# A hybrid decoder's MLPs: each pair of feature tiles of the first product alternates with the second product of four earlier tiles

## Chip, core and metric

One core of one Trainium2 chip runs the whole kernel. The metric is the device time of one launch in microseconds (us). Three runs of the kernel before the change took 1593.59, 1597.19 and 1599.14 us; the median is 1597.19 us.

## The reference

The program is one step of a two-layer decoder trunk on T = 544 tokens (512 of a prompt, 8 x 4 of samples), width 1024, in float32. Layer 0 mixes with mLSTM and GLA heads, layer 1 with an SSD scan; each mixer is followed by a squared-ReLU MLP with 4096 features. The change is in the two MLPs alone:

```
def _mlp(x, w1, w2):
    return jnp.square(jax.nn.relu(x @ w1)) @ w2

x = _layernorm(DN_ALPHA * x + _mlp(x, w1[l], w2[l]), g, b)     # for both layers
```

## The kernel before

Everything is held transposed: features on the 128 partitions, tokens along the row, in two halves of 272 tokens. The 4096 features of an MLP are 32 tiles of 128. A product in float32 is made of three matmuls: each operand x is split into a rounded part (hi, a cast on ScalarE) and the rest (lo, a subtraction on VectorE), and hi*hi, hi*lo, lo*hi are added up in PSUM. So each weight block, 128 x 1024, is loaded by a DMA from SyncE's queue into a buffer `wraw` (three of them), cast by ScalarE into `whi` (L148) and subtracted by VectorE into `wlo` (L149).

The first product makes hidden tiles (function `act`, L474): ReLU on ScalarE (L478), the square on VectorE or GpSimd (L479), then the split into `hh` and `hlo` (`split`, L262 to 264: cast on ScalarE, subtraction on VectorE). Eight hidden tiles are kept at a time (`bufs=8`). The second product (`dense`, L328) takes them as its moving operand: for an output block b of 128 features and one token half, 3 matmuls for each hidden tile run into one PSUM bank (`psd`, three banks), and VectorE adds the sum into the residual stream `xf` (`residual`, L370 for the first group, L372 after).

`mlp` (L432) goes through four groups c of eight feature tiles. In group 0 the first six tiles (`HEADM`) are plain products, done for token half 0 of all six and then for half 1. Meanwhile `take_sums` (L444) prepares sums of the activations, t1 to t4. All the other tiles come in pairs (`pair`, L482): seven quarter products of 12 matmuls each in place of eight, as in Strassen's method, with weight sums that GpSimd forms (`_pair` of the weight stream, L172 to 175, into `wsum`) and that are split like the rest (L183, L184). The quarters run in the order a11, s2, s3, s1, a12, a22, s4. A pair m gives four half tiles. Tile m+1, half 1 (called c22) is complete after the fourth quarter, tile m, half 0 after a12, tile m+1, half 0 (c21) after a22, tile m, half 1 (c12) after s4. The half from a12 is squared on VectorE, the other three on GpSimd.

After the pairs of a group the eight output blocks follow, each over the group's eight hidden tiles (24 matmuls for each half): `phase(8, hrhs, KT, residual(c == 0))`. In group 3 the last seven blocks go as one group, half by half, and the layer norm starts behind each half.

What sets the order of the work: TensorE keeps the order of the code (`manual_schedule`). For the other engines a scheduler writes a fixed order for each engine while the program is built, and each engine then executes its own queue strictly in that order. The weight stream (`WeightStream`, L101) prepares blocks ahead: `next` (L192) emits as many blocks as fit in six buffers (`HLB` = 5 and `HLM` = 1), where a pair counts as three; a pair's fourth piece (a22) has a single buffer of its own, and so has `wsum`.

Of the kernel before, what the change touches and what calls it, by code (L numbers as in the profile page):

```python
# [33 lines left out]

W = dict(dec=12, gates=400, sc=16, lev=12, v=8, kd=10, out=33, end=12, c0=15, u=11, s=16, ml=12, dt=238, sg=72, sx=14, sq=26, so=48, l0=12, l1=12, v0=60, v1=55)
LEVELS = (64, 32, 16, 8, 4, 2, 1)

# [63 lines left out]
class WeightStream:  # L101
# [14 lines left out]

    @staticmethod
    def _size(block):
        return 1 if len(block) == 2 else 3
# [4 lines left out]
    def _emit(self, between=None):  # L124
        nc = self.nc
        phase, *srcs = self.blocks[self.done]
        self.done += 1
        if len(srcs) == 2:
            with self.tc.high_priority():
                self.tiles.append(self._pair(phase, *srcs))  # L130
            return
        src, = srcs
        _, kt, _ = src.shape
        pool = self._pool(phase)
        with self.tc.high_priority(), ExitStack() as after:

            for i in self.cut:
                if i is not None:
                    after.enter_context(self.tc.issue_after(i))
            self.cut = [None, None]  # L140
            w = self.raw.tile([P, kt, P], F32, tag="wraw", name="wraw")
            hi = pool.tile([P, kt, P], F32R, tag="whi", name="whi")
            lo = pool.tile([P, kt, P], F32R, tag="wlo", name="wlo")
# [8 lines left out]
            self.tiles.append((hi, lo))  # L152

    def _pool(self, phase):
        if phase == self.extra_phase:
# [53 lines left out]
def trunk_kernel(ctx, tc, a, stages=("ab", "mlp0", "ssd", "mlp1")):  # L209
# [19 lines left out]
    for st in stages:  # L229
        if st == "ab":  # L230
            for w in [a["ab_gate"]] + [a["ab_in"][b] for b in range(24)]:
                ws.plan("ab", w)
            for b in range(8):
                ws.plan("abo", a["ab_out"][b])
        elif st == "ssd":
            for w in [a["ssd_dt"]] + [a["ssd_in"][b] for b in range(40)]:
                ws.plan("ssd", w)
            for w in [a["ssd_out"][b] for b in range(16)]:
                ws.plan("ssdo", w)
        else:  # L240
            l = int(st[3])
            for c in range(4):
                n = HEADM if c == 0 else 0
                for b in range(n):
                    ws.plan(st, a["mlp_w1"][l, c * 8 + b])
                for b in range(n, 8, 2):
                    ws.plan(st, a["mlp_w1"][l, c * 8 + b], a["mlp_w1"][l, c * 8 + b + 1])
                for b in range(8):
                    ws.plan(st, a["mlp_w2"][l, c, b])


    xf = [None, None]
# [179 lines left out]
    def mlp(l, phase_, outer, xp, out):  # L432
# [29 lines left out]
        for c in range(4):  # L462
            hid = {}

            def place(m):
                if m not in hid:
                    hid[m] = (pool.tile([P, T], F32R, tag="hh", name="hh", bufs=8),
                              pool.tile([P, T], F32R, tag="hlo", name="hlo", bufs=8))
                return hid[m]

            def hr():
                return pool.tile([P, TH], F32, tag="hr", name="hr", bufs=6)

            def act(m, hf, x, E, r=None):  # L474
                c0, c1 = HALVES[hf]
                h = place(m)
                r = hr() if r is None else r
                S.activation(r, x, AF.Relu)  # L478
                E.tensor_tensor(r, r, r, ALU.mult)  # L479
                split(h[0][:, c0:c1], h[1][:, c0:c1], r)  # L480

            def pair(m):  # L482
                w = ws.next()
                pa, pb, pc, pe = (x[:, :TH] for x in (psd.tile([P, 512], F32, tag="d", name="psd"), pm("psd"),
                                                      psd.tile([P, 512], F32, tag="d", name="psd"), pm("psd")))
                hp = tc.high_priority
                z, c22, c21, c12 = (hr() for _ in range(4))
                quarter(w["a11"], bt["b11"], pa, True)
                with hp():
                    S.copy(z, pa)  # L490
                quarter(w["s2"], bt["t2"], pb, True)
                with hp():
                    V.tensor_tensor(z, z, pb, ALU.add)
                quarter(w["s3"], bt["t3"], pc, True)
                with hp():
                    V.tensor_tensor(c22, z, pc, ALU.add)  # L496
                quarter(w["s1"], bt["t1"], pe, True)
                with hp():
                    V.tensor_tensor(c22, c22, pe, ALU.add)
                quarter(w["a12"], bt["b21"], pa, False)  # L500
                with hp():
                    act(m + 1, 1, c22, G, c22)
                    act(m, 0, pa, V)
                quarter(w["a22"], bt["t4"], pc, False)
                with hp():
                    V.tensor_tensor(c21, z, pc, ALU.add)
                    act(m + 1, 0, c21, G, c21)
                quarter(w["s4"], bt["b22"], pe, False)
                with hp():
                    V.tensor_tensor(c12, z, pe, ALU.add)  # L510
                    act(m, 1, c12, G, c12)

            def hrhs(k, hf):
                c0, c1 = HALVES[hf]
                return hid[k][0][:, c0:c1], hid[k][1][:, c0:c1]

            if c == 0:
                phase(HEADM, xrhs, KT, lambda m, hf, ps: act(m, hf, ps, V), head=HEADM)
                take_sums()
            for m in range(HEADM if c == 0 else 0, 8, 2):  # L520
                if (c, m) == (3, 6):
                    ws.lend(None, None, 0)
                pair(m)
            if c < 3:
                phase(8, hrhs, KT, residual(c == 0))
            else:
                own.close()
                ws.lend(outer.enter_context(tc.tile_pool(name="hlx" + phase_, bufs=HLX, reuse_waits="tile")), phase_, HLX)
                phase(8, hrhs, KT, residual(False, xp, out is not None), tail=TAIL,
                      after=lambda hf: launch(layernorm(hf, 2 * l + 1, xp, out)))  # L530


    def ab(pool):
# [1300 lines left out]
```

## Time and profile before

| what | value |
|---|---|
| median of the three runs | 1597.19 us |
| the profiled execution, its own time | 1592.68 us |
| its span, first to last instruction | 1591.0 us |
| mean granted TensorE clock | 0.983 |
| matmuls of the program | 11621 |
| first MLP's products, us from the span's start | about 331 to 717 |
| second MLP's products | about 1209 to 1574 |

The span is the time between the first and the last instruction of the profiled execution; its own time is 1.7 us longer. In the profile PE is TensorE's matmuls, PEld its weight loads, DVE is VectorE, ACT is ScalarE, POOL is GpSimd, SP is SyncE. A row such as "psd<-hh,whi" names the tile written, then those read. In the rows of groups, "x1024 | 297.6, 291 | 6.3 <-ACT hh" reads: 1024 instructions, 297.6 us busy, 291 ns each, and 6.3 us in which the engine idled just before them, ended mostly by ScalarE's write of `hh`. Matmuls overlap: the duration of one is longer than the step from one start to the next.

### The profile page before, as it was taken

The numbers are of one execution on the slowest core, as the hardware profiler recorded it, in microseconds if no ns is written. First come the engines' busy times: TensorE is split into PE (matmuls) and PEld (weight loads), VectorE is DVE, ScalarE is ACT, GpSimd is POOL, SyncE is SP. The second block draws the span as 40 slices with busy tenths as digits, with TensorE's granted clock in tenths as the row PEclk, the third lists the DMA queues.
The fourth block names the chain that finished last, engine by engine and source line by source line (L and its number), as shares of the span: only waits on it lengthen the run. The fifth ranks groups of instructions, "written<-read, shape, count | busy, mean of one in ns | idle before, by whom it ended". The sixth has DMA issues, their size and how long they took to land.

```text
span 1591.0 us, 29243 instructions
## 1 busy us (share of the span) xinstructions
PE 1504.7 (95%) x11621; PEld 1446.0 (91%) x11621; DVE 1060.7 (67%) x1871; ACT 734.6 (46%) x1569; POOL 586.7 (37%) x603
## 2 busy tenths in 40 slices
PE   8899999989999999999799999999898999999997
PEld 7799989989989999999787788899888999999996
DVE  4963566777383655757798978667669647474654
ACT  6543555344251433525585666645234435162433
POOL 0320323353242434344353463543245233343421
PEclk9999999999999999999999999999999999999999
DMA  6121122503142241415447667363221414132221
GB/s 221 58 81 63 44 94 87 176 26 119 38 138 70 59 146 41 154 50 187 101 130 242 207 176 251 94 217 118 67 61 46 133 41 133 54 113 87 67 80 57
DMA packets 81488, 172.10 MB, mean 108 GB/s; under 512 B 14696, under 2 KB 39144, under 8 KB 81096
## 3 DMA queue, kind: packets, MB, share of 16 engines
q1 hardware_dynamic: 45384, 141.20, 28.0%
q10 hardware_dynamic: 33376, 18.42, 4.6%
q0 software_dynamic: 2592, 10.62, 1.7%
q8 instruction: 91, 1.49, 0.4%
q14 instruction: 45, 0.37, 0.1%
HBM read 153.48 MB, written 16.73 MB: 107 GB/s over the span
## 4 chain that ended last, share of the span: by engine, by line
PE 61%; DVE 15%; POOL 5%; ACT 4%; DMA 4%; issue 4%; ACTq 1%; SPq 0%; DVEq 0%; POOLq 0%
PE psd L339 46%; PE psd L429 6%; DVE wlo L149 3%; DMA wraw<-mlp_w 2%; DVE wlo L184 1%; DVE hlo L264 1%; DVE hr L479 1%; ACT whi L148 1%; POOL hr L479 1%; PE num L657 1%; DVE xf L412 1%; PE yp L1436 1%; PE it L1483 1%; DVE xl L420 1%; POOL xf L421 1%
## 5 line engine op out<-in xcount | busy, mean ns | idle before, releaser
L339 PE MATMUL psd<-xh,whi 128*128 128x272 f32 x1504 | 450.4, 299 | 6.7 <-ACT xh L263 5.0
L339 PE MATMUL psd<-xh,wlo 128*128 128x272 f32 x1504 | 445.7, 296 | 0.4 <-DVE wlo L149 0.4
L339 PE MATMUL psd<-xl,whi 128*128 128x272 f32 x1504 | 444.9, 296 | 0.5 <-DVE xl L264 0.5
L339 PE MATMUL psd<-hh,whi 128*128 128x272 f32 x1024 | 297.6, 291 | 6.3 <-ACT hh L263 6.3
L339 PE MATMUL psd<-hlo,whi 128*128 128x272 f32 x1024 | 297.6, 291 | 6.1 <-DVE hlo L264 5.8
L339 PEld LDWEIGHTS psd<-xh,whi 128*128 128x128 f32 x1504 | 289.2, 192 | 14.0 <-ACT xh L263 5.6
L339 PE MATMUL psd<-hh,wlo 128*128 128x272 f32 x1024 | 296.8, 290 | 0.0
L339 PEld LDWEIGHTS psd<-xl,whi 128*128 128x128 f32 x1504 | 289.4, 192 | 7.0 <-issue 3.8
L339 PEld LDWEIGHTS psd<-xh,wlo 128*128 128x128 f32 x1504 | 288.9, 192 | 4.8 <-issue 3.0
L149 DVE TENSOR_TENSOR wlo<-wraw,whi 128x1024 fp32r<-128x1024 f32 (+1 forms) x169 | 217.1, 1288 | 72.2 <-ACT whi L148 71.1
L148 ACT CAST whi<-wraw 128x1024 fp32r<-128x1024 f32 (+1 forms) x169 | 173.3, 1031 | 151.7 <-PE psd L339 115.7
L339 PEld LDWEIGHTS psd<-hlo,whi 128*128 128x128 f32 x1024 | 194.2, 190 | 7.9 <-DVE hlo L264 7.8
L339 PEld LDWEIGHTS psd<-hh,whi 128*128 128x128 f32 x1024 | 194.2, 190 | 7.9 <-ACT hh L263 7.9
L339 PEld LDWEIGHTS psd<-hh,wlo 128*128 128x128 f32 x1024 | 194.2, 190 | 0.1
L372 DVE TENSOR_TENSOR xf<-xf,psd 128x272 f32<-128x272 f32 x112 | 48.6, 435 | 145.8 <-PE psd L339 145.8
L479 POOL TENSOR_TENSOR hr<-hr 128x272 f32<-128x272 f32 x78 | 83.6, 1079 | 149.7 <-ACT hr L478 149.5
L429 PE MATMUL psd<-xh,whi 128*128 128x272 f32 x416 | 120.8, 290 | 4.1 <-DVE hr L496 4.0
L429 PE MATMUL psd<-xh,wlo 128*128 128x272 f32 x416 | 119.8, 288 | 0.0
L429 PE MATMUL psd<-xl,whi 128*128 128x272 f32 x416 | 119.6, 288 | 0.0
L172 POOL TENSOR_TENSOR wsum<-wraw 128x512 f32<-128x512 f32 x26 | 34.6, 1331 | 230.4 <-DVE wlo L184 161.5
L183 ACT CAST whi<-wsum 128x1024 fp32r<-128x1024 f32 x52 | 54.5, 1048 | 140.1 <-PE psd L339 120.2
L183 ACT CAST whi<-wraw 128x512 fp32r<-128x512 f32 (+1 forms) x52 | 43.4, 834 | 111.5 <-PE psd L339 39.1
(449 smaller groups left out, 3124.9 us busy)
## 6 DMA issues: line engine op xcount, KB each, us to landing
wraw<-mlp_w SPq DMA_DIRECT2D x128, 512.0 KB, 3.8
wraw<-ssd_in SPq DMA_DIRECT2D x40, 512.0 KB, 4.3
wraw<-ab_in SPq DMA_DIRECT2D x24, 512.0 KB, 3.6
h<-h SPq DMA_DIRECT2D x32, 256.0 KB, 4.1
h0n<-h0n SPq DMA_DIRECT2D x16, 512.0 KB, 5.0
E<-d_cs ACTq DMA_DIRECT2D x16, 512.0 KB, 5.0
s_h<-h0n POOLq DMA_DIRECT2D x16, 512.0 KB, 4.2
wraw<-ssd_out SPq DMA_DIRECT2D x16, 512.0 KB, 3.7
```

The lines of the kernel that those rows point to most:

```text
L148: nc.scalar.copy(hi[:, r], w[:, r])
L149: nc.vector.tensor_tensor(lo[:, r], w[:, r], hi[:, r].bitcast(F32), ALU.subtract)
L172: G.tensor_tensor(sr[:, 0], a21, a22, ALU.add)
L183: self.cut[0] = nc.scalar.copy(hi, x).ins
L184: self.cut[1] = nc.vector.tensor_tensor(lo, x, hi.bitcast(F32), ALU.subtract).ins
L264: V.tensor_tensor(lo, src, hi.bitcast(F32), ALU.subtract)
L339: last[0] = TE.matmul(ps[:, :TH], wt[:, k, :], rt, start=i == 0, stop=i == n - 1).ins
L372: V.tensor_tensor(x, x, ps, ALU.add)
L412: V.scalar_tensor_tensor(xk, xk, gk, rs, ALU.mult, ALU.mult)
L420: V.scalar_tensor_tensor(xl[hf][:, k], xk, bk, xh[hf][:, k].bitcast(F32), ALU.add, ALU.subtract)
L429: last[0] = TE.matmul(ps, wt[:, k], bt[:, k], start=first and n == 0, stop=n == 11, skip_group_check=not first).ins
L479: E.tensor_tensor(r, r, r, ALU.mult)
```

## The change

The groups of eight are given up. A table `MLP` lists the order of one MLP: "out" is the second product over the n hidden tiles from tile m on, for a list of output blocks; "pair" is a pair of the first product. Its core is that pair m+4 stands between the first four output blocks of tiles m to m+3 and the other four, and pair m+6 behind these.

- The first six tiles (plain products) are followed at once by four output blocks over these six tiles, then come pair 6, the other four blocks, pair 8, all eight blocks over tiles 6 and 7, and pair 10.
- From tile 8 on: four blocks over tiles 8 to 11, pair 12, four blocks, pair 14, and so on to tile 20, then pairs 24, 26 (each before two blocks of tiles 20 to 23), 28 and 30, one behind the other, and the last eight blocks over tiles 24 to 31 as before.
- A second product over four tiles has 12 matmuls for a block and half, over two tiles 6; so there are more sums for VectorE to add into `xf`: 112 in an MLP in place of 64.
- Two output blocks over four tiles (or four over two) share one weight buffer of 128 x 1024: two (or four) DMAs, one cast, one subtraction.
- In a pair, a22 now stands before a12: c21 is complete after the fifth quarter, tile m, half 0, after the sixth, and the steps of c22 are written ahead of a22.

The instructions of TensorE are the same in number.

```
+    two = [(0, 1), (2, 3), (4, 5), (6, 7)]
+    one = [(b,) for b in range(8)]
+    o = [("out", 0, 6, one[:4]), ("pair", 6), ("out", 0, 6, one[4:]), ("pair", 8),
+         ("out", 6, 2, [(0, 1, 2, 3), (4, 5, 6, 7)]), ("pair", 10)]
+    for m in range(8, 20, 4):
+        o += [("out", m, 4, two[:2]), ("pair", m + 4), ("out", m, 4, two[2:]), ("pair", m + 6)]
+    return o + [("out", 20, 4, two[:2]), ("pair", 24), ("out", 20, 4, two[2:3]), ("pair", 26),
+                ("out", 20, 4, two[3:]), ("pair", 28), ("pair", 30), ("last", 24, 8, one)]
...
-            step = kt if between is None else kt // len(between)
-            for k in range(0, kt, step):
+            n = kt * len(srcs)
+            step = n if between is None else n // len(between)
+            for k in range(0, n, step):
                 r = slice(k, k + step)
-                nc.sync.dma_start(out=w[:, r], in_=src[:, r])
+                if between is not None:
+                    nc.sync.dma_start(out=w[:, r], in_=srcs[0][:, r])
+                else:
+                    for i, src in enumerate(srcs):
+                        nc.sync.dma_start(out=w[:, i * kt:(i + 1) * kt], in_=src)
...
                 with hp():
                     V.tensor_tensor(c22, c22, pe, ALU.add)
-                quarter(w["a12"], bt["b21"], pa, False)
-                with hp():
-                    act(m + 1, 1, c22, G, c22)
-                    act(m, 0, pa, V)
+                    act(m + 1, 1, c22, G, c22)
                 quarter(w["a22"], bt["t4"], pc, False)
                 with hp():
                     V.tensor_tensor(c21, z, pc, ALU.add)
                     act(m + 1, 0, c21, G, c21)
+                quarter(w["a12"], bt["b21"], pa, False)
+                with hp():
+                    act(m, 0, pa, V)
...
-            for m in range(HEADM if c == 0 else 0, 8, 2):
-                if (c, m) == (3, 6):
+        for kind, m, *r in MLP:
+            if kind == "pair":
+                if m == 30:
                     ws.lend(None, None, 0)
                 pair(m)
-            if c < 3:
-                phase(8, hrhs, KT, residual(c == 0))
+                continue
+            n, blocks = r
...
+            ev = residual(m == 0)
+            for bs in blocks:
+                w = ws.next()
+                for b, wb in zip(bs, w if len(bs) > 1 else [w]):
+                    for hf in range(2):
+                        dense(wb, hrhs(m), n, hf, lambda h, p, b=b: ev(b, h, p))
```

The order of instructions shows the change at two places. The first is VectorE's queue around the end of a pair whose tiles the next second product needs. Before, this is the last pair of group 1 in the first MLP (its sums are `hr_5192` to `hr_5194`, made by L506, L510 and rows above; `hr_5267` is its half from a12; L149 is a weight block's split, L372 adds an output sum into `xf`):

```order
L149 TENSOR_TENSOR wlo_5314<-wraw_5312,whi_5313 128x1024
L479 TENSOR_TENSOR hr_5267<-hr_5267 128x272
L506 TENSOR_TENSOR hr_5193<-hr_5191,psd_5189 128x272
L264 TENSOR_TENSOR hlo_5260<-hr_5192,hh_5259 128x272
L510 TENSOR_TENSOR hr_5194<-hr_5191,psd_5190 128x272
L264 TENSOR_TENSOR hlo_5266<-hr_5267,hh_5265 128x272
L149 TENSOR_TENSOR wlo_5320<-wraw_5318,whi_5319 128x1024
L264 TENSOR_TENSOR hlo_5260<-hr_5193,hh_5259 128x272
L264 TENSOR_TENSOR hlo_5266<-hr_5194,hh_5265 128x272
L372 TENSOR_TENSOR xf0_3092<-xf0_3092,psd_5324 128x272
```

Now, at pair 10 of the first MLP (`hr_4950` is c22, `hr_4951` c21, `hr_4952` c12, `hr_5042` the half from a12; L204 splits weights of the next pair, L168 those of an output block, L393 adds into `xf`; L523 comes after a22, L530 after s4):

```order
L523 TENSOR_TENSOR hr_4951<-hr_4949,psd_4947 128x272
L204 TENSOR_TENSOR wlo_5086<-wraw_5066,whi_5085 128x512
L285 TENSOR_TENSOR hlo_5006<-hr_4950,hh_5005 128x272
L204 TENSOR_TENSOR wlo_5078<-wsum_5068,whi_5077 128x1024
L530 TENSOR_TENSOR hr_4952<-hr_4949,psd_4948 128x272
L499 TENSOR_TENSOR hr_5042<-hr_5042 128x272
L285 TENSOR_TENSOR hlo_5006<-hr_4951,hh_5005 128x272
L168 TENSOR_TENSOR wlo_5091<-wraw_5089,whi_5090 128x1024
L285 TENSOR_TENSOR hlo_5041<-hr_5042,hh_5040 128x272
L285 TENSOR_TENSOR hlo_5041<-hr_4952,hh_5040 128x272
L393 TENSOR_TENSOR xf0_3092<-xf0_3092,psd_5096 128x272
L393 TENSOR_TENSOR xf1_3097<-xf1_3097,psd_5110 128x272
```

The half from a12 (`hlo_5266` before, the first `hlo_5041` now) stood ahead of the last weight split and now stands behind two of them, one of the next pair (`wlo_5078`) and one of an output block (`wlo_5091`). ScalarE's queue at the same place is, before:

```order
L478 ACTIVATE hr_5267<-psd_5187 128x272
L263 CAST hh_5259<-hr_5192 128x272
L263 CAST hh_5265<-hr_5267 128x272
L148 CAST whi_5319<-wraw_5318 128x1024
L478 ACTIVATE hr_5193<-hr_5193 128x272
L478 ACTIVATE hr_5194<-hr_5194 128x272
L263 CAST hh_5259<-hr_5193 128x272
L263 CAST hh_5265<-hr_5194 128x272
```

and now (L203 casts weights of the next pair, L167 those of an output block, L498 is the ReLU, L284 the cast of a hidden half):

```order
L498 ACTIVATE hr_4951<-hr_4951 128x272
L203 CAST whi_5077<-wsum_5068 128x1024
L498 ACTIVATE hr_5042<-psd_4945 128x272
L284 CAST hh_5005<-hr_4951 128x272
L167 CAST whi_5090<-wraw_5089 128x1024
L498 ACTIVATE hr_4952<-hr_4952 128x272
L284 CAST hh_5040<-hr_5042 128x272
L284 CAST hh_5040<-hr_4952 128x272
```

The ReLU of the half from a12 (`hr_5042`) has a weight cast ahead of it, and its own cast into `hh_5040` another.

The second place is VectorE's queue at the end of the six plain tiles of the first MLP. Before, `hr_4117` is half 1 of the sixth tile, `hr_4151` and on belong to pair 6, which follows:

```order
L264 TENSOR_TENSOR xl1_76<-tsum_4122,xh1_74 128x1088
L264 TENSOR_TENSOR hlo_3904<-hr_4087,hh_3903 128x272
L149 TENSOR_TENSOR wlo_4143<-wraw_4141,whi_4142 128x1024
L479 TENSOR_TENSOR hr_4117<-hr_4117 128x272
L493 TENSOR_TENSOR hr_4151<-hr_4151,psd_4148 128x272
L264 TENSOR_TENSOR hlo_3936<-hr_4117,hh_3935 128x272
L496 TENSOR_TENSOR hr_4152<-hr_4151,psd_4149 128x272
```

Now (`hr_4104` is that half; `wlo_4178`, `wlo_4190` and `wlo_4182` are weights of pair 6, L391 adds the first output sum):

```order
L204 TENSOR_TENSOR wlo_4178<-wraw_4168,whi_4177 128x1024
L499 TENSOR_TENSOR hr_4074<-hr_4074 128x272
L204 TENSOR_TENSOR wlo_4190<-wraw_4170,whi_4189 128x512
L285 TENSOR_TENSOR xl1_76<-tsum_4109,xh1_74 128x1088
L285 TENSOR_TENSOR hlo_3891<-hr_4074,hh_3890 128x272
L499 TENSOR_TENSOR hr_4104<-hr_4104 128x272
L391 SCALAR_TENSOR_TENSOR xf0_3092<-xf0_3092,psd_4128 128x272
L204 TENSOR_TENSOR wlo_4182<-wsum_4172,whi_4181 128x1024
L285 TENSOR_TENSOR hlo_3923<-hr_4104,hh_3922 128x272
L391 SCALAR_TENSOR_TENSOR xf1_3097<-xf1_3097,psd_4148 128x272
```

The last hidden half (`hlo_3936` before, `hlo_3923` now) stands behind splits of weights in both; but what follows the plain tiles on TensorE is now the product that reads this half, where before pair 6, which does not read it, came first.

More of the change, by code (lines that the diff above doesn't have):

```diff
@@ L151, in _emit @@
                     between[k // step]()
-            self.tiles.append((hi, lo))
+            t = [(hi[:, i:i + kt], lo[:, i:i + kt]) for i in range(0, n, kt)]
+            self.tiles.append(t if len(srcs) > 1 else t[0])
     def _pool(self, phase):
@@ new lines, in mlp, with place, hr, act @@
+        hid = {}
+        def place(m):
+            if m not in hid:
+                hid[m] = (pool.tile([P, T], F32R, tag="hh", name="hh", bufs=8),
+                          pool.tile([P, T], F32R, tag="hlo", name="hlo", bufs=8))
+            return hid[m]
+        def hr():
+            return pool.tile([P, TH], F32, tag="hr", name="hr", bufs=6)
+        def act(m, hf, x, E, r=None):
+            c0, c1 = HALVES[hf]
+            h = place(m)
+            r = hr() if r is None else r
+            S.activation(r, x, AF.Relu)
+            E.tensor_tensor(r, r, r, ALU.mult)
+            split(h[0][:, c0:c1], h[1][:, c0:c1], r)
@@ L533, in ab @@
+            if blocks[-1][-1] == 7:
+                for k in range(m, m + n):
+                    del hid[k]
     def ab(pool):
```

117 lines of the change are left out of this document (52 added, 65 removed).

## The prediction, made blind

> **What bounds the kernel now.** I read the page first, then the busy times of the two MLP stretches, then TensorE's waits, then these waits in the timeline.
>
> ```profile
> PE 1504.7 (95%) x11621; PEld 1446.0 (91%) x11621; DVE 1060.7 (67%) x1871; ACT 734.6 (46%) x1569; POOL 586.7 (37%) x603
> ```
> ```profile
> 331.00:717.00 386.00, 373.79 (x2918) 370.32 (x2918) 240.10 (x359) 151.52 (x262) 145.31 (x126) 0.99 0.28 85
> 1209.00:1574.00 365.00, 358.19 (x2833) 355.80 (x2832) 221.43 (x328) 139.30 (x240) 134.84 (x110) 1.00 0.26 82
> ```
>
> TensorE is the bound, in the MLPs too (columns: stretch, its length, PE, PEld, DVE, ACT, POOL, clock, DMA share, GB/s). VectorE is busy 240 of 386 us there, the DMA engines 28%. The change leaves the number of matmuls, so it can only remove or add waits of TensorE, or change its clock. The waits, of the whole kernel (columns: total us, times, longest):
>
> ```profile
> PE psd L339 <- ACT hh L263: 6.3, 7, 1.6
> PE psd L339 <- DVE hlo L264: 5.8, 4, 1.9
> PE psd L429 <- DVE hr L496: 4.0, 5, 1.1
> ```
>
> The first two rows are the eight places where a second product follows its group's last pair, the third lies inside pairs. One of the eight, in the timeline:
>
> ```profile
> 471.93 0.29 PE L339 MATMUL psd<-hh,whi 128*128 128x272 f32 x1
> ...
> 474.45 0.29 PE L339 MATMUL psd<-hh,wlo 128*128 128x272 f32 x1
> 476.35 0.39 PE L339 MATMUL psd<-hh,whi 128*128 128x272 f32 x1 [1.61 <-ACT hh L263]
> ```
>
> The second product begins at 471.93, and its 21st matmul at 474.45: one step is 0.126 us. The 22nd, the first that reads the pair's c21, waits until 476.35, 4.42 us after the pair's end. A step would have been 0.126, so the wait costs 1.77 us where the row shows 1.61: add 0.16 to each wait.
>
> Such waits have a second price, seen in windows of 3.41 us, the grid on which the granted clock changes (it is the third number from the end):
>
> ```profile
> 474.72:478.13 3.41, 1.72 (x12) 1.49 (x12) 1.95 (x4) 0.85 (x3) 1.72 (x2) 1.00 0.77 245
> 478.13:481.54 3.41, 3.41 (x17) 3.41 (x16) 0.00 (x0) 0.00 (x0) 0.00 (x0) 0.50 0.08 32
> 662.45:665.86 3.41, 1.91 (x13) 1.61 (x13) 3.14 (x5) 1.79 (x3) 1.63 (x2) 1.00 0.80 269
> 665.87:669.28 3.41, 3.41 (x17) 3.41 (x16) 2.10 (x2) 1.94 (x2) 0.00 (x0) 0.50 0.75 253
> 570.29:573.70 3.41, 2.31 (x18) 2.31 (x19) 2.18 (x5) 0.42 (x1) 0.74 (x1) 1.00 0.77 246
> 573.70:577.11 3.41, 3.41 (x29) 3.41 (x28) 1.25 (x2) 1.05 (x1) 0.00 (x0) 1.00 0.09 36
> ```
>
> After a window in which TensorE was idle 1.5 us or more, the next was granted half the clock and ran 17 matmuls in place of 27 (3.41 / 0.126): 10 x 0.126 = 1.3 us lost. After an idle 1.1 us it was not.
>
> **The change, part by part.** *Removed.* The three rows sum to 16.1 us in 16 waits; with 0.16 for each, 18.7. The waits of the last second product in each MLP stay, since pair 30 is followed by eight blocks over eight tiles as now:
>
> ```profile
> 663.01 0.40 PE L339 MATMUL psd<-hh,whi 128*128 128x272 f32 x1 [0.47 <-ACT hh L263]
> 664.44 0.39 PE L339 MATMUL psd<-hlo,whi 128*128 128x272 f32 x1 [1.03 <-DVE hlo L264]
> 1526.21 0.39 PE L339 MATMUL psd<-hh,whi 128*128 128x272 f32 x1 [0.49 <-ACT hh L263]
> 1527.63 0.39 PE L339 MATMUL psd<-hlo,whi 128*128 128x272 f32 x1 [1.03 <-DVE hlo L264]
> ```
>
> That is 3.0 + 4 x 0.16 = 3.7. So 15.0 us goes, if no pair waits inside any more: the L496 waits came with pairs back to back, when VectorE had no pause; now only 28 and 30 touch. (a22 adds to the bank of s3 and now comes one quarter, 1.51 us, behind the fourth's start, not two; should VectorE be late with that bank, a pair would wait up to the 1.1 us of the row's longest.) The half-clock stretch at 478 goes too: 1.3. Removed: 16.3 us.
>
> *Added, first: four second products in each MLP read the pair right before them* (over tiles 8, 12, 16 and 20, after pairs 10, 14, 18 and 22), and with four tiles instead of eight they reach it sooner. Six matmuls, 0.76 us, and the seventh reads the half from a12, the eighth its `hlo`: due 0.88 us after the pair's end. When is it ready? The steps:
>
> ```profile
> L183 ACT CAST whi<-wsum 128x1024 fp32r<-128x1024 f32 x52 | 54.5, 1048 | 140.1 <-PE psd L339 120.2 <-POOL wsum L173 18.2 <-PE psd L429 1.1
> L478 ACT ACTIVATE hr<-psd 128x272 f32<-128x272 f32 x25 | 9.8, 391 | 5.3 <-PE psd L339 4.3 <-PE psd L429 1.0
> L263 ACT CAST hh<-hr 128x272 fp32r<-128x272 f32 x64 | 26.1, 418 | 29.2 <-POOL hr L479 18.3 <-DVE hr L479 10.8
> 364.12 1.21 DVE L184 TENSOR_TENSOR wlo<-wsum,whi 128x1024 fp32r<-128x1024 f32 x1
> 365.25 0.43 DVE L479 TENSOR_TENSOR hr<-hr 128x272 f32<-128x272 f32 x1
> 365.61 0.43 DVE L264 TENSOR_TENSOR hlo<-hr,hh 128x272 fp32r<-128x272 f32 x1
> ```
>
> On VectorE a weight split takes a step of 1.13 us (364.12 to 365.25), a 272-wide one 0.36. Both queues execute in the order shown above. Let the pair end at 0; its sixth quarter (a12) ends 12 steps earlier, at -1.51, and gives back the weight buffer that the next pair's split needs. ScalarE casts that until -0.45, does the ReLU (0.39) until -0.06 and c21's cast (0.42) until 0.36. The output block's cast follows; its buffer is given back by the last quarter, at 0: 0.36 to 1.41. VectorE: the pair's weight split -0.45 to 0.68, c12's sum to 1.04, the square of the half from a12 to 1.40, c21's `hlo` to 1.76, the output block's split to 2.89, and only then the `hlo` that TensorE waits for, done at 3.3. Between engines some 0.05 us more at each step. So it waits until 3.4, 2.5 us; c12 is due 1.4 us after that and, with GpSimd's square of 1.08 us (row below) ending about 3.0, is split by 3.9: it adds nothing. Eight places: 20.0 us. Lower bound: without the two weight splits the half would be in time and c12's chain would remain: sum 0.36, ReLU 0.39, square 1.08, cast 0.42, `hlo` 0.44, 2.7 us and four handovers of 0.05, against the 2.27 due (18 steps): 0.65 us. Upper: 3.3, with splits at the mean of 1.39 us that POOL's company gives them and a slower square. I take 2.5, since each row stands in the order as said.
>
> ```profile
> L479 POOL TENSOR_TENSOR hr<-hr 128x272 f32<-128x272 f32 x78 | 83.6, 1079 | 149.7 <-ACT hr L478 149.5
> L184 DVE TENSOR_TENSOR wlo<-wsum,whi 128x1024 fp32r<-128x1024 f32 x52 | 72.4, 1392 | 18.9 <-ACT whi L183 18.9
> ```
>
> *Second: the first output block follows the six plain tiles.* Its second half reads tile 5, half 1, after 33 steps, 4.3 us with the `hlo`. In the profile this half was split here, where nobody needed it yet:
>
> ```profile
> 365.48 0.29 PE L429 MATMUL psd<-xh,whi 128*128 128x272 f32 x1
> 373.24 0.44 DVE L264 TENSOR_TENSOR hlo<-hr,hh 128x272 fp32r<-128x272 f32 x1
> 1233.96 0.28 PE L429 MATMUL psd<-xh,whi 128*128 128x272 f32 x1
> 1240.45 0.44 DVE L264 TENSOR_TENSOR hlo<-hr,hh 128x272 fp32r<-128x272 f32 x1
> ```
>
> That is 8.2 and 6.9 us after the plain tiles' end. Ahead of it VectorE will have about 0.6 us less to do: six splits of 1024 columns are replaced by four of 768 (three quarters of 1.13 each, an estimate), two of 1024 and one of 512. So 7.6 and 6.3: waits of 3.3 and 2.0, 5.3 us. Bounds: 1 and 12 for both, since the pair's sums now come from GpSimd in this stretch and a split of them stands ahead in the queue.
>
> *Third, small.* VectorE adds 48 sums more in each MLP, and two output blocks' sums can wait behind a weight split of 1.13:
>
> ```profile
> L372 DVE TENSOR_TENSOR xf<-xf,psd 128x272 f32<-128x272 f32 x112 | 48.6, 435 | 145.8 <-PE psd L339 145.8
> ```
>
> 48 x 0.435 = 21 us on 240 of 386: hidden, as TensorE has three banks, and a group of 12 matmuls lasts 1.51, so a sum may be 3.0 us late. Over tiles 6 and 7 a group lasts only 0.76 and 1.5 us are left: a weight split and two `hlo` there push it 0.65 past, 1.3 us for both MLPs. The DMAs carry the same bytes in more pieces on SyncE's queue:
>
> ```profile
> wraw<-mlp_w SPq DMA_DIRECT2D x128, 512.0 KB, 3.8
> ```
>
> At 28% share I add nothing: a block lands in 3.8 us and is asked for about a pair (10.6 us, 84 steps) ahead. If that cover went, ScalarE's casts would wait for `wraw`, and TensorE for them.
>
> *Fourth, the clock.* A wait of 2.5 us shows as about 2.3 us idle, and puts the 1.7 us of the row at 474 into one window for (3.41 - 2.3 + 2 x 0.6) / 3.41 = 0.68 of its positions: 8 x 0.68 x 1.3 = 7.1 us. The Trainium skill, page "TensorE: Matmul & The Clock Gate", section "HAM oscillation — how this bites in real kernels", states the rule as no idle gap above about 3.4 us, by which waits of 2.5 us would cost no clock; the rows at 478 and 665 speak against it.
>
> Sum: 20.0 + 5.3 + 1.3 + 7.1 - 16.3 = +17.4 us. On the profiled execution's own 1592.7 that gives 1610.1; it ran 4.5 us under the median of the runs, and I predict on the median: 1597.2 + 17.4 = 1614.6.
>
> **Rivals.**
> - *Faster: weights are ready early, and only c12's chain is left.* VectorE pauses 38% of the stretch, and the sums' row shows it waiting for TensorE 146 us; if the two splits were out of the way, eight waits of 0.65 (5.2), 1.0 at the plain tiles, 1.3 and no half clock against the 16.3 give -8.8: 1588.4. Against: both buffers come back from the very pair that is running. It decides below (16.3 - 5.3 - 1.3) / 8 = 1.2 us a wait. Chance 0.20.
> - *Nothing gained or lost.* Waits of about 1.1 us, half of the two splits hidden: 8.8 + 5.3 + 1.3 and some clock, 0.9, equal 16.3: 1597.2. Against it stands the same order. Chance 0.13.
> - *The clock stays whole*, as in the second MLP, whose row shows 1.00 although second products waited there: 17.4 - 7.1 = +10.3, 1607.5. Chance 0.12. The page of the Trainium skill on the clock gate, named above, has this case.
> - *The first output block waits for GpSimd's sums*, 6 us in each MLP, 12 instead of 5.3: +6.7 more, 1621.3. For it: a split of those sums stands ahead of the half; against: before, the sums were early. Chance 0.10.
> - *As forecast*, 0.45.
>
> **How the numbers follow.** About 0.3%, 4.8 us, is what a measurement can tell from no change here. Faster 0.20, same 0.13, slower 0.12 + 0.10 + 0.45 = 0.67. The range reaches down to the faster rival's own figure and up to where waits of 3.3 us (+6.4) and the GpSimd case (+6.7) come together with two more half-clock windows: 1588 to 1630.
>
> **What would show it.** In the changed kernel's waits, hidden tiles (`hh`, `hlo`) should hold TensorE after pairs 10, 14, 18, 22 for some 2.5 us each, more in sum than the 12.1 us of now, with the `hlo` right behind the output block's split; the row for waits inside pairs should be gone; more half-clock windows should stand in the MLPs; the first output block should wait once for the sixth tile. It is wrong if those waits are under 1.2 us, or if TensorE waits for weights or PSUM banks instead.

## The result, and the profile after

| | before | after |
|---|---|---|
| median of four runs each, us | 1595.39 | 1635.10 |
| lowest and highest run, us | 1592.62 to 1599.14 | 1632.21 to 1640.29 |
| profiled execution, own time, us | 1592.68 | 1632.44 |
| mean granted clock | 0.983 | 0.967 |

The changed kernel is slower: the ratio is 1.0251, with a 95% interval of 1.0212 to 1.0290, some 40 us. The forecast had the sign, +17.4 us, and a range up to 1630.0; the time lies above it.

The two MLP stretches after the change (from the first quarter product behind the plain tiles, or the first second product, to the last second product; columns as in the prediction):

```profile
358.23:734.02 375.79, 350.76 (x2634) 345.33 (x2632) 228.00 (x360) 132.12 (x223) 131.61 (x113) 0.95 0.27 85
1242.99:1615.31 372.32, 347.36 (x2634) 342.25 (x2633) 219.15 (x348) 128.22 (x219) 125.84 (x104) 0.95 0.26 80
```

And the same stretches before, cut at the same two events:

```profile
365.48:713.04 347.56, 337.31 (x2633) 334.14 (x2632) 206.44 (x311) 130.53 (x221) 125.70 (x109) 0.99 0.29 90
1233.96:1574.00 340.04, 333.23 (x2634) 330.84 (x2633) 196.47 (x297) 125.43 (x216) 120.47 (x100) 1.00 0.27 86
```

So the MLPs lost 28.2 and 32.3 us, 60.5 together, while the span grew by only 39.6: outside of them 20.9 us was won. The matmuls are the same, their clock is not (0.95 where it was 0.99 and 1.00). What TensorE waited for, whole kernel:

```profile
PE psd L360 <- DVE hlo L285: 24.6, 16, 4.5
PE psd L360 <- ACT hh L284: 21.7, 14, 1.9
PE var L427 <- DVE lnq L423: 4.8, 4, 1.6
PE mu L412 <- DVE lns L399: 3.7, 2, 2.0
```

The two hidden-tile rows have grown from 12.1 to 46.3 us. The row for waits inside pairs (L496, 4.0 us before) is gone, as forecast. The layer norms' rows have shrunk; before, they were 9.7 and 8.6 us, the figures that come back further below where pair 6 is put back.

To split the loss I went through the starts of the MLPs' matmuls: a step over 0.26 us is a wait, less the 0.126 of a step; a step of 0.16 to 0.26 us is one at half clock. In the two MLPs together:

| us, both MLPs | before | after | forecast of the difference |
|---|---|---|---|
| waits | 22.7 | 63.8 | +11.6 |
| steps at half clock, over 0.126 | 5.2 | 24.6 | +5.8 |
| outside the MLPs | | -20.9 | 0 |

Of the waits after, counting steps over 0.4 us (shorter ones of about 0.39 us are the slow steps just behind a wait), 32.0 us lie at the eight dependent places (six of 3.58, pair 22's of 5.8 and 4.7), 16.4 at the two first output blocks (8.1 and 8.3), 6.6 at the last second products, 2.2 at the products over tiles 6 and 7, `out(6,2)`.

**One dependent place**, pair 10 of the first MLP, in the timeline (start, duration). The second product starts at 450.70:

```profile
450.70 0.28 PE L360 MATMUL psd<-hh,whi 128*128 128x272 f32 x1
...
453.35 0.39 PE L360 MATMUL psd<-hh,whi 128*128 128x272 f32 x1 [1.75 <-ACT hh L284]
455.15 0.59 PE L360 MATMUL psd<-hlo,whi 128*128 128x272 f32 x1 [1.41 <-DVE hlo L285]
```

The half was split 4.45 us after the pair's end, where the forecast had 3.4. ScalarE, VectorE and GpSimd there:

```profile
449.50 0.43 ACT L498 ACTIVATE hr<-hr 128x272 f32<-128x272 f32 x1
449.83 1.03 ACT L203 CAST whi<-wsum 128x1024 fp32r<-128x1024 f32 x1
```
```profile
450.89 1.23 DVE L204 TENSOR_TENSOR wlo<-wsum,whi 128x1024 fp32r<-128x1024 f32 x1 [0.83 <-PE psd L450]
...
453.09 1.22 DVE L168 TENSOR_TENSOR wlo<-wraw,whi 128x1024 fp32r<-128x1024 f32 x1
454.22 0.88 DVE L285 TENSOR_TENSOR hlo<-hr,hh 128x272 fp32r<-128x272 f32 x1
```
```profile
447.79 1.35 POOL L499 TENSOR_TENSOR hr<-hr 128x272 f32<-128x272 f32 x1 [7.39 <-ACT hr L498]
453.07 1.73 POOL L499 TENSOR_TENSOR hr<-hr 128x272 f32<-128x272 f32 x1 [2.43 <-ACT hr L498]
```

From the cast of the next pair's sums on, the order is the one of the forecast, step by step. Two sizes are not. That cast starts 0.87 us before the pair's end, not 1.51, since ScalarE first casts c22 (whose square GpSimd took 1.35 us for) and does c21's ReLU, which the forecast left out: +0.64. And the last split takes 0.88 in place of 0.43 us while GpSimd squares: +0.45. Together 3.4 + 1.1 = 4.5.

### The profile page after: what moved, and what is told of

It is laid out like the page before. It is cut to its first block, busy times and chain, and to the rows that moved or that the text cites. A ratio compares the mean times of both kernels' runs of the same rounds, so it can differ in the third digit from the quotient of the medians.

```text
span 1630.6 us, 29432 instructions
## 1 busy us (share of the span) xinstructions
PE 1523.4 (93%) x11621; PEld 1462.1 (90%) x11621; DVE 1094.7 (67%) x1971; ACT 735.7 (45%) x1573; POOL 587.9 (36%) x603
## 4 chain that ended last, share of the span: by engine, by line
PE 72%; DVE 11%; ACT 4%; DMA 4%; issue 2%; POOL 2%; ACTq 1%; DVEq 0%; POOLq 0%; SPq 0%
PE psd L360 49%; PE psd L450 14%; DVE wlo L168 2%; DMA wraw<-mlp_w 1%; DVE hlo L285 1%; DVE wlo L204 1%; PE yp L1468 1%; ACT whi L167 1%; PE num L689 1%; PE sp L1446 1%; PE it L1515 1%; ACT whi L203 1%; DVE xl L1582 1%; PE var L427 1%; PE snum L779 0%
## 5 line engine op out<-in xcount | busy, mean ns | idle before, releaser
L360 PE MATMUL psd<-hlo,whi 128*128 128x272 f32 x1024 | 309.1, 302 | 24.6 <-DVE hlo L285 24.6
L360 PE MATMUL psd<-hh,whi 128*128 128x272 f32 x1024 | 308.8, 302 | 24.2 <-ACT hh L284 21.7
L360 PE MATMUL psd<-hh,wlo 128*128 128x272 f32 x1024 | 306.3, 299 | 0.0
L167 ACT CAST whi<-wraw 128x1024 fp32r<-128x1024 f32 (+2 forms) x173 | 174.5, 1012 | 224.0 <-PE psd L360 199.1
L168 DVE TENSOR_TENSOR wlo<-wraw,whi 128x1024 fp32r<-128x1024 f32 (+2 forms) x173 | 214.0, 1238 | 73.1 <-ACT whi L167 71.7
L360 PEld LDWEIGHTS psd<-hh,whi 128*128 128x128 f32 x1024 | 204.0, 199 | 30.0 <-ACT hh L284 25.2
L360 PEld LDWEIGHTS psd<-hlo,whi 128*128 128x128 f32 x1024 | 204.1, 199 | 28.5 <-DVE hlo L285 28.3
L360 PEld LDWEIGHTS psd<-hh,wlo 128*128 128x128 f32 x1024 | 204.4, 200 | 0.1
L393 DVE TENSOR_TENSOR xf<-xf,psd 128x272 f32<-128x272 f32 x208 | 89.0, 433 | 156.2 <-PE psd L360 156.2
L203 ACT CAST whi<-wsum 128x1024 fp32r<-128x1024 f32 x52 | 54.3, 1044 | 103.6 <-PE psd L450 79.6
L203 ACT CAST whi<-wraw 128x1024 fp32r<-128x1024 f32 (+1 forms) x52 | 43.4, 835 | 102.2 <-PE psd L360 91.1
```

The costliest lines, as they stand in the source:

```text
L203: self.cut[0] = nc.scalar.copy(hi, x).ins
L360: last[0] = TE.matmul(ps[:, :TH], wt[:, k, :], rt, start=i == 0, stop=i == n - 1).ins
L393: V.tensor_tensor(x, x, ps, ALU.add)
```

## The experiments

Each kernel is timed side by side with the kernel before. That kernel's median was 1595.4 us beside the changed kernel and 1590.6, 1590.0 and 1588.7 us in the three later sets of runs, so I compare ratios. The times expected of kernels made from the changed kernel start from its 1635 us, without this shift of some 5 us. Mechanisms are read from the traces.

**Is it the dependent places?** The table is shifted by one pair:

```
-        o += [("out", m, 4, two[:2]), ("pair", m + 4), ("out", m, 4, two[2:]), ("pair", m + 6)]
+        o += [("out", m, 4, two[:2]), ("pair", m + 6), ("out", m, 4, two[2:]), ("pair", m + 8)]
```

with pair 12 right behind pair 10 at the start, and one pair less at the end.

> The changed kernel with its table shifted by one pair, so that from tile 8 on no second product reads the pair that ran just ahead of it; groups of four, pieces of weights, inner order of a pair and number of sums stay. Theory (the loss is the eight dependent places and the half clock behind them): in the changed kernel's trace these places waited 32.0 us and were followed by eight stretches of 6.83 us at half clock, 55 of the MLPs' 75 us, which cost about 18 us; both go, 1635 - 50 = about 1585 us, with at most 10 us of new waits, 1585 to 1597. Rival (the 48 more sums per MLP, the smaller groups or the smaller weight pieces are the cost): they all stay, 1625 us or more.

Measured 1594.32 us, ratio 1.0027 (1.0004 to 1.0050). Its waits:

```profile
PE psd L361 <- DVE xf L394: 11.6, 10, 2.5
PE psd L361 <- DVE hlo L286: 11.2, 6, 4.5
PE psd L361 <- ACT hh L285: 7.2, 5, 1.9
```

From 1.0251 to 1.0027 is 2.24%, 36 us: nearly the whole loss, with all the small groups, pieces and additional sums still there. Half clock in the MLPs fell from 75.1 us of windows to 20.5. Not all of the 50 us came back: VectorE's sums (`xf`), which held TensorE for 1.6 us in the changed kernel, now hold it for 11.6 us, mostly at the short products over tiles 6 and 7. The rival falls.

**The order inside a pair**, alone in each direction. In the changed kernel a12 goes back ahead of a22 (inner); in the kernel before, a22 goes ahead of a12 (bswap):

```
+            quarter(w["a12"], bt["b21"], pa, False)
+            with hp():
+                act(m, 0, pa, V)
             quarter(w["a22"], bt["t4"], pc, False)
...
-            quarter(w["a12"], bt["b21"], pa, False)
-            with hp():
-                act(m, 0, pa, V)
```

> The changed kernel with the old order inside a pair (a12 ahead of a22). Theory: the order of a22 and a12 has no large part in the loss; a12's half is then done a quarter (1.5 us) later in its chain only where VectorE is late, so the dependent places wait about the same: now c21's half is the late one instead. 1630 to 1640. Rival (the new inner order is what makes the dependent places wait): waits fall by over 1 us at each of eight places, below 1625.

> The kernel before with the new inner order of a pair alone (a22 ahead of a12), groups of eight tiles kept. Theory: no part of the loss comes from it; within 4 us of the kernel before, 1591 to 1599. Rival (it adds waits inside pairs, since a22 adds to the bank of s3 one quarter sooner): up to 1.1 us at each of 26 pairs, 1605 to 1622.

Inner: 1622.10 us, ratio 1.0205 (1.0165 to 1.0245). Its dependent places wait 2.9 us each, 23.6 us together where the changed kernel has 32.0, and its last second products 3.9 us where that has 6.6. The time is below the 1625 of the rival, but by the ratio, on 1595.4, it is 1628, and the interval overlaps that of the changed kernel. So the traces show the new inner order to cost some 11 us of waits there; what it costs in time is likely a part of the loss and not shown. Bswap: 1608.46 us, ratio 1.0116 (1.0081 to 1.0152). Here the theory falls. The waits inside pairs of this kernel:

```profile
PE psd L429 <- DVE hr L496: 8.0, 9, 2.3
PE psd L429 <- ACT whi L148: 5.0, 2, 3.1
```

4.0 before, 13.0 now; more is added after the groups (`hlo` 10.3 us, 5.8 before). The first row shows that a22, where pairs follow each other, reaches the bank of s3 before VectorE has read it (L496); the second is one wait at pair 6 of each MLP. The prediction had this wait, priced it at nothing because the changed kernel keeps its pairs apart, and there it is indeed absent.

**The first output block and the layer norm.** Pair 6 is put ahead of the first output product, as before the change:

```
-    o = [("out", 0, 6, one[:4]), ("pair", 6), ("out", 0, 6, one[4:]), ("pair", 8),
+    o = [("pair", 6), ("out", 0, 6, one), ("pair", 8),
```

> The changed kernel with pair 6 back ahead of the first output product (all eight blocks over tiles 0 to 5 together behind it). Theory (the sums that GpSimd makes for pair 6 cost TensorE where they land: in the layer norm ahead of the MLP before, at the end of the plain tiles after): the first output block's 16.4 us of waits and some half clock go, and the layer norm's waits of 5.3 and 6.4 us with their half clock come back, about 12 to 19 us; within 6 us of the changed kernel, 1629 to 1641. Rival (the first block waits only since it stands right behind tile 5, and the layer norms got shorter for another reason): the 16 us go and nothing comes back, about 1617.

Measured 1630.10 us, ratio 1.0248 (1.0213 to 1.0284), not told apart from the changed kernel. In the trace, taken from the fastest of the four runs (1623.88 us), the MLPs are 21.7 us shorter, and 13.1 us are back outside. The layer norms' waits, the same two figures as in the kernel before:

```profile
PE var L428 <- DVE lnq L424: 9.7, 4, 6.1
PE mu L413 <- DVE lns L400: 8.6, 3, 5.0
```

GpSimd's queue in the first layer norm of the kernel before shows why: four sums of pair 6's weights stand between those of the norm (the last of them and its neighbours):

```profile
325.27 0.74 POOL L378 TENSOR_TENSOR lns<-lns,xf 128x272 f32<-128x272 f32 x1
325.98 1.25 POOL L175 TENSOR_TENSOR wsum<-wraw,wsum 128x512 f32<-128x512 f32 x1
327.20 0.74 POOL L378 TENSOR_TENSOR lns<-lns,xf 128x272 f32<-128x272 f32 x1
```

The four take 5.6 us there, and VectorE waits for the norm's next sum behind them:

```profile
327.98 0.44 DVE L378 TENSOR_TENSOR lns<-lns,xf 128x272 f32<-128x272 f32 x1 [5.01 <-POOL lns L378]
```

In the changed kernel pair 6 stands four blocks later in the stream of weights, its sums start at 360.97, and the norm goes through. So the change moved a cost, from the norm to the end of the plain tiles. What it costs there is measured with two kernels in which pair 6's splits read raw weights, so that both leave out the sums from the product: one makes no sums on GpSimd, the other makes them and nobody reads them.

```
-        for x in (r[0], sr[:, 0:2]..., sr[:, 2:4]..., a22):
+        s21, s34 = (r[1], r[0]) if bare else (sr[:, 0:2]..., sr[:, 2:4]...)
+        for x in (r[0], s21, s34, a22):
```

> The changed kernel without the four sums that GpSimd makes of pair 6's weights; its four split instructions of the same sizes read the raw weights in their place. Left out: these sums in both MLPs. Theory (VectorE is slowed by GpSimd's company there): the first output block's waits, 8.1 us in each MLP, fall to about 3, its 10 us of half clock shrink, about 1620. Rival (the queue's order alone makes the wait): the splits of the pair and their place stay, so do the waits, 1630 to 1637.

> As the kernel without pair 6's sums, but GpSimd still makes them, and nobody reads them: the same splits wait for nothing of GpSimd's and run beside it. Left out: the use of these sums. If GpSimd's company is the cause, the first block's waits come back here, 6 to 8 us in each MLP, and VectorE's instructions take 1.5 to 2.4 us there; if the wait came from splits that wait for their sums, this kernel is as fast as the one without.

The first blocks waited 4.2 and 4.5 us without the sums, 8.3 in both MLPs with them unread, 8.1 and 8.3 in the changed kernel (steps over 0.4 us, less 0.126 each). GpSimd and VectorE there in the changed kernel:

```profile
360.97 2.06 POOL L192 TENSOR_TENSOR wsum<-wraw 128x512 f32<-128x512 f32 x1 [6.40 <-DMA wraw<-mlp_w]
362.98 1.47 POOL L194 TENSOR_TENSOR wsum<-wraw 128x512 f32<-128x512 f32 x1
364.41 1.71 POOL L193 TENSOR_TENSOR wsum<-wsum,wraw 128x512 f32<-128x512 f32 x1
366.20 2.20 POOL L195 TENSOR_TENSOR wsum<-wraw,wsum 128x512 f32<-128x512 f32 x1
```
```profile
360.65 1.23 DVE L204 TENSOR_TENSOR wlo<-wraw,whi 128x1024 fp32r<-128x1024 f32 x1 [0.51 <-PE psd L360]
361.80 1.53 DVE L499 TENSOR_TENSOR hr<-hr 128x272 f32<-128x272 f32 x1
363.25 1.75 DVE L204 TENSOR_TENSOR wlo<-wraw,whi 128x512 fp32r<-128x512 f32 x1
364.92 2.35 DVE L285 TENSOR_TENSOR xl<-tsum,xh 128x1088 fp32r<-128x1088 f32 x1
367.19 1.50 DVE L285 TENSOR_TENSOR hlo<-hr,hh 128x272 fp32r<-128x272 f32 x1
```

The same VectorE instructions without GpSimd's:

```profile
362.57 0.44 DVE L502 TENSOR_TENSOR hr<-hr 128x272 f32<-128x272 f32 x1
362.92 0.69 DVE L207 TENSOR_TENSOR wlo<-wraw,whi 128x512 fp32r<-128x512 f32 x1
363.52 1.28 DVE L288 TENSOR_TENSOR xl<-tsum,xh 128x1088 fp32r<-128x1088 f32 x1
```

and with the unread ones:

```profile
363.29 1.53 DVE L500 TENSOR_TENSOR hr<-hr 128x272 f32<-128x272 f32 x1
364.74 1.76 DVE L205 TENSOR_TENSOR wlo<-wraw,whi 128x512 fp32r<-128x512 f32 x1
366.42 2.35 DVE L286 TENSOR_TENSOR xl<-tsum,xh 128x1088 fp32r<-128x1088 f32 x1
```

That settles half of the wait: GpSimd's company makes 4 us of the 8, by lengthening VectorE's instructions. The other half stays without it, with pair 6's splits still in VectorE's queue there; that their place in the queue makes it was not tested by itself. The expected times were missed. The kernels ran 1629.75 and 1627.49 us, ratios 1.0247 (1.0216 to 1.0278) and 1.0235 (1.0205 to 1.0265), not told apart from each other or from the changed kernel. The 7.7 us of waits that the first one saves show as 5.7 us in its MLPs; the clock took part: 78.5 us of half-clock windows in its MLPs, 44.4 in the kernel with unread sums, whose dependent places wait just as long.

**The clock.** 24 matmuls, overwritten by the group's first, are put into each dependent wait:

```
+        if warm is not None:
+            for _ in range(24):
+                TE.matmul(ps[:, :TH], hi[:, k0, :], warm, start=True, stop=True)
```

> The changed kernel with 24 more matmuls (3.0 us, their result overwritten) ahead of the second products over tiles 8, 12, 16 and 20 in each MLP: they lie in the time for which these products wait (3.6 to 5.8 us), so that TensorE stays busy. Theory (idle time of 1.7 us or more in a window halves the clock of the next two): the waits shrink to about 0.6 us where they were 3.6, all but the longer ones after pair 22 lose their half clock; time 1635 - 15 = about 1620. Rival (the half clock has another cause than the idle time, or the weights come later since the matmuls hold the buffer): 1635 or more.

Measured 1617.29 us, ratio 1.0172 (1.0135 to 1.0208): 0.8% or 13 us faster with more work. None of the eight places is followed by half clock now, where all were. Windows of 3.41 us behind pair 10, in the changed kernel:

```profile
450.69:454.11 3.42, 1.31 (x9) 0.88 (x7) 3.22 (x5) 2.45 (x6) 1.04 (x1) 1.00 0.51 152
454.11:457.52 3.41, 2.37 (x10) 2.37 (x11) 1.87 (x4) 0.42 (x1) 0.69 (x1) 0.50 0.52 154
457.52:460.93 3.41, 3.41 (x17) 3.41 (x16) 0.44 (x1) 0.00 (x0) 2.91 (x3) 0.50 0.00 0
```

and with the additional matmuls:

```profile
450.41:453.83 3.42, 3.42 (x30) 3.42 (x29) 2.59 (x6) 3.27 (x7) 0.64 (x1) 1.00 0.55 153
453.83:457.24 3.41, 3.03 (x25) 2.81 (x24) 2.86 (x5) 0.70 (x2) 1.73 (x1) 1.00 0.31 68
```

So the half clock behind these waits comes from their idle time. One dependent place touched two windows, 2.1 and 1.0 us idle, and the window after each ran at half clock. How much idle time it takes stays open, since the kernel with unread sums has two equal places with different outcomes:

```profile
451.48:454.90 3.42, 1.68 (x13) 1.34 (x11) 2.76 (x5) 2.91 (x6) 1.00 (x2) 1.00 0.46 153
454.90:458.31 3.41, 2.00 (x9) 1.91 (x9) 2.26 (x4) 0.42 (x1) 1.15 (x1) 0.50 0.51 137
...
553.91:557.33 3.42, 1.68 (x13) 1.39 (x11) 2.71 (x5) 2.96 (x6) 0.99 (x2) 1.00 0.54 153
557.33:560.74 3.41, 2.00 (x15) 1.86 (x15) 2.37 (x4) 0.42 (x1) 1.20 (x1) 1.00 0.50 125
```

Both first windows are idle for 1.74 us; one is followed by half clock, the other is not.

**GpSimd's squares.** In the changed kernel ScalarE makes the squares of c22, c21 and c12:

```
-            E.tensor_tensor(r, r, r, ALU.mult)
+            if E is G:
+                S.activation(r, r, AF.Square)
+            else:
+                E.tensor_tensor(r, r, r, ALU.mult)
```

> The changed kernel with the three squares of a pair that GpSimd makes (c22, c21, c12) made by ScalarE in their place. Theory (half of what the dependent wait exceeds the forecast comes from GpSimd's squares beside VectorE: 0.88 us for the split of a half where alone it takes 0.43, squares of 1.1 to 1.7 us): each of the eight dependent waits falls from 3.6 to about 2.5 us, time 1622 to 1630. Rival (ScalarE, with three more instructions of 0.4 us a pair ahead of the weights' casts, is late with them): waits as long as now or longer, 1635 or more.

Measured 1617.69 us, ratio 1.0172 (1.0148 to 1.0196). The dependent place behind pair 10 waits 2.72 us (two steps of 1.68 and 1.30, less 0.126 each) in place of 3.58. Six more wait as long; the last one, behind pair 22 of the second MLP, still waits 4.9 us. Several half-clock windows go too: 34.1 us of them are left in the MLPs, 75.1 in the changed kernel. The pair's end, ScalarE's cast and the last splits there:

```profile
453.58 0.28 PE L360 MATMUL psd<-hh,whi 128*128 128x272 f32 x1
452.29 1.03 ACT L203 CAST whi<-wsum 128x1024 fp32r<-128x1024 f32 x1
456.33 0.79 DVE L285 TENSOR_TENSOR hlo<-hr,hh 128x272 fp32r<-128x272 f32 x2
```

The cast starts 1.29 us before the pair's end, where it was 0.87, and two splits take 0.79 us, where one took 0.88. The theory holds for the waits. The gain, 0.8% or 13 us by the ratios, is at the upper end of what was expected (5 to 13 us).

**A version that beats both.** Groups of four from the first tile, each pair one place ahead of its need:

```
+    o = []
+    for m in range(0, 24, 4):
+        o += [("out", m, 4, two[:2]), ("pair", m + 6), ("out", m, 4, two[2:]), ("pair", m + 8)]
+    return o + [("pair", 30), ("last", 24, 8, one)]
```

> Second products over four tiles at a time throughout (0 to 3, 4 to 7, ..., 20 to 23, the last over eight as before), each pair put between them one place sooner than the changed kernel, so that no second product reads the pair right before it and the first one does not read the sixth plain tile. Theory (a second product loses only where it reads what was just made): beside the shifted kernel's gain the first output block's 8 us in each MLP with about 4 us of half clock go, and the waits of out(6,2) for sums (4.8 us in the shifted kernel): 1594 - 25 = about 1570 us, faster than the kernel before. Rival (VectorE's time while GpSimd makes pair 6's sums is short wherever they land): a wait of like size opens at another place of the first groups, 1585 to 1597.

Measured 1585.36 us, ratio 0.9963 (0.9945 to 0.9981): faster than before, but by the rival's figure. A new wait opened: TensorE waited 4.5 and 2.3 us in the first MLP and 8.0 us in the second for the ReLU that frees its bank. Three variants followed: pair 6 two output blocks later (`two[:3]` ahead of it), the same with a12 ahead of a22, and the same with squares on ScalarE.

> As the kernel with groups of four throughout, but pair 6 comes behind six of the first group's output blocks, not four, and pair 8 behind all eight. There, the ReLUs of the last two plain tiles stood in ScalarE's queue behind the cast of sums that GpSimd had not made yet, and TensorE waited 7.0 and 8.1 us for the bank. Theory (one output block more ahead in the stream of weights moves these sums past the plain tiles, to where nothing of VectorE's is due for some us): these waits go, with about 3 us of half clock in each MLP, 1585 - 15 - 5 = about 1567 us. Rival (they only move on, to the first output sums or to pair 6 itself, which now comes 3 us later): 1580 to 1590.

> The kernel with pair 6 behind six output blocks and the old order inside a pair (a12 ahead of a22). Theory: without dependent places and with pairs apart, the inner order has nothing to hold up, within 3 us of the kernel with the new inner order. Rival: the old order costs less as it did in the groups of eight (bswap, 18 us more with the new) and in the changed kernel (13 us): 5 us or more faster.

> The kernel with pair 6 behind six output blocks and the squares of pairs on ScalarE. Theory: TensorE waits for these squares nowhere but after the last pair (3.3 us an MLP) and VectorE's spare time is not what bounds; within 4 us of the same kernel with squares on GpSimd. Rival (VectorE, slowed by GpSimd in every pair, is behind everywhere): over 6 us faster.

What was expected of the first of them rests on a misreading that the trace corrects. ScalarE's queue, with groups of four throughout:

```profile
358.76 0.39 ACT L496 ACTIVATE hr<-psd 128x272 f32<-128x272 f32 x1
367.68 0.42 ACT L282 CAST hh<-hr 128x272 fp32r<-128x272 f32 x1 [8.53 <-DVE hr L497]
```

It was not a weight cast that held ScalarE for 8.5 us, but the cast of a hidden half that waited for VectorE's square, again on VectorE in GpSimd's company. Measured: 1583.13 us, ratio 0.9940 (0.9918 to 0.9962), a time inside its rival's range, since only part of the wait went (5.6 us an MLP is left); with a12 first 1578.45 us, 0.9921 (0.9903 to 0.9938); with squares on ScalarE 1583.69 us, 0.9964 (0.9949 to 0.9980), within the 4 us of its theory. The kernel with a12 first is the fastest, 0.8% under the kernel before; against the one with the new inner order it gains 4.7 us, more than its theory allows and under its rival's 5 (the 13 us that this rival quotes for the changed kernel are 0.5%, 7 us, by the ratios), and the two intervals overlap, so the inner order's worth here stays open.

## Why the prediction was wrong

- **Bound and removed waits: right in kind.** TensorE stayed the bound, the waits inside pairs went. The last second products were to keep their 3.7 us and took 6.6; with the old order inside a pair they took 3.9, so the new order is what added to them.
- **The eight dependent waits: mechanism right, size wrong**, 32.0 us for 20.0. The queue order was read correctly from the weight cast on; that cast's start on ScalarE was 0.64 us later and the last split 0.45 us longer. With the squares on ScalarE, 0.42 of the first and all of the second were gone, so GpSimd's squares made 0.87 of the 1.1 us; the other 0.22 are steps of ScalarE's queue ahead of the cast that were left out. Pair 22's two waits were longer still. The upper bound given, 3.3 us a wait, was below the truth; it was made from VectorE's mean split with GpSimd's company, not from the chain shifted as a whole. The shifted table shows what the places cost.
- **First output block: 16.4 for 5.3.** The rival at 12 us named the right engine, but its mechanism, a wait for the sums, was wrong: unread sums cost as much. What the step left out is that GpSimd's four sums lengthen what VectorE does beside them: without them the blocks waited 8.7. The remaining 3.4 us over the forecast are not attributed.
- **The clock: by a little, the term that failed most**, 24.6 us of half-clock steps in the MLPs against 5.2 before, +19.4 for a net forecast of +5.8. At the eight places alone it was 17.2 for 7.1. I counted at most one halved window a wait, by its share of positions. Each place was followed by two, 6.83 us, and in the changed kernel the places lie 51.2 to 51.4 us apart (the last of the first MLP included), close to 15 windows, so that each met the grid within 0.5 us of the same position, and all of them badly. Nor does the rule hold that 1.5 us idle in a window halves the next: 1.74 us did it once and once did not. The Trainium skill, page "TensorE: Matmul & The Clock Gate", section "What's actually happening", has the window running free of the kernel; the equal waits with 0 to 6.83 us of half clock in the kernel with unread sums agree. Its other rule, in the section "HAM oscillation — how this bites in real kernels", no idle gap above about 3.4 us, isn't enough by these rows: gaps of 1.8 and 1.4 us within one wait of 3.6 us did it.
- **Outside the MLPs: a step that was not made.** I priced nothing there, yet the move of pair 6 in the stream took its sums out of GpSimd's queue in the layer norms. 20.9 us came from there; 13.1 of it went back with pair 6, the remaining 8 are not attributed. Half clock could hold most of them: outside the MLPs 49.9 us of such windows stand in the trace before and 36.9 in that of the kernel with pair 6 back, which is at most 6.5 us of time.
- **Hidden things were hidden** in the changed kernel: 48 more sums an MLP (1.6 us of waits for `xf`), the DMA's pieces, the smaller groups. The shifted kernel has them all, and the first blocks' waits too, and costs 0.3%, though there the sums hold TensorE for 11.6 us.

The errors partly cancelled: +60.5 us in the MLPs for 17.4, -20.9 outside for 0. Of the 43.1 us missed in the MLPs, the dependent places made 12.0, the first output blocks 11.1, the last second products 2.9 and the clock 13.6.

## What to carry to other kernels

When two products alternate, put one more piece of independent work between a producer and its reader than the handover seems to need: the shift by one pair was worth 36 us of the same instructions. Price a wait together with the clock behind it, and count the windows it can touch. And when a step moves in a prefetch stream, price what it leaves behind and where its helper instructions land, on GpSimd's queue too.

## What the runs showed of the hardware

- VectorE and GpSimd took turns, instruction by instruction. In the changed kernel's rows at the first output block, GpSimd's first sum (360.97) ends 1.15 us after VectorE's split that was running (361.88); VectorE's square, started at 361.80, ends 0.30 us after that sum (363.03); GpSimd's next sum ends 1.12 us after that square (363.33), and so on: each duration holds a wait for the other's instruction. The Trainium skill, page "SBUF — State Buffer", section "Who interferes with whom", states that a VectorE instruction with two inputs in SBUF contends with a GpSimd instruction that reads SBUF, and calls their shared ports an exclusive lock. The rows agree, and the price here was 4 us of VectorE's time for four sums.
- Keeping TensorE busy with matmuls that nobody reads made the kernel 13 us faster.
